# Eight merge-gate tiles as two seven-product block steps inside the second attention, with sums and scalings on GpSimd

## The chip, the cores and the metric

One NeuronCore of a Trainium2 chip runs the whole kernel as one program. The metric is the time of one execution on the device, in microseconds; the kernel's time is the median of three runs. The engines are named as in the profile: PE is TensorE (matmuls), PEld its weight loads, DVE is VectorE, ACT is ScalarE, POOL is GpSimd, and SP is SyncE, which here only issues DMAs.

## The reference

The layer works on 512 tokens of width 1024: a half-weighted feed-forward stage, a token mixer, a second half-weighted feed-forward stage, each between norms. The change lies in the token mixer, which projects the normed tokens `h` once with a wide matrix `w_in`, runs two attentions on slices of the result, and merges them with two gates:

```python
proj = h @ w_in
q_n, kv_n, g_n, qkv_d, merge = jnp.split(proj, np.cumsum(sizes)[:-1].tolist(), axis=-1)
...
o_nsa = nsa_attention(...)                       # first attention, 8 heads of 64
o_dil = dilated_attention(q, k, v)               # second attention, 3 groups of 4 heads of 64
y_nsa = o_nsa.reshape(B, S, Q_NSA) @ w_nsa_o
y_dil = o_dil.reshape(B, S, DIL_OUT) @ w_dil_o
g_a, g_b = jnp.split(merge, 2, axis=-1)          # 1024 columns each
y = jax.nn.sigmoid(g_a) * y_nsa + jax.nn.sigmoid(g_b) * y_dil
return y @ w_mix_out
```

In the second attention each of the three groups has its own window and dilation (128 by 1, 512 by 4, 2048 by 16). The groups' outputs are combined with weights that come from all three softmax denominators:

```python
for gidx, (window, dil) in enumerate(DIL_CONFIGS):
    o, lse = banded_attention(strided(q), strided(k), strided(v), 1, window // dil, dil, slopes[gidx])
    ...
w = jax.nn.softmax(jnp.stack(lses), axis=0)
o = jnp.sum(w[..., None] * jnp.stack(outs).astype(jnp.float32), axis=0)
```

## The kernel before

Every fp32 matrix product is done as three fp32r matmuls: each operand is split into a high part (ACT casts it, L149) and a rest (DVE subtracts, L150), and `mm3` issues high x high, high x rest and rest x high (L172 to L174). For a weight the parts are the tiles `whi` and `wlo`, three buffers each; the tokens' parts, with the feature in the partitions, are `xhl_t` (views `xh`, `xl`, `xht`, `xlt`). Weights come from DRAM into `raw` tiles of 1 MB, of which there are three. PSUM has eight banks under four tags: three S, two T, one V, two F. Tiles of 128x512 have tags of their own with a fixed count (SP 11, x 8, PT 8, Q, KA, KB and V 4 each, ring 3, W and of 2). The order of instructions on each engine is set when the kernel is built: a list planner takes the instructions in program order as their priority and places each on its engine by a cost model; `issue_after(i)` keeps an instruction behind instruction `i`. SP's queue of DMAs is in such an order too, and so is POOL's.

The mixer runs in these steps.

`nsa` is the first attention: 16 pairs of head and branch; scores on PE, softmax on DVE and ACT, the scaling of the probabilities mostly on POOL (L1180), transposes and value products on PE. The heads' outputs are folded (`fold`, L1207) into four tiles `of`, and each is split at once into `oh` and `ol`, which are the stationary-side input of the output projection later.

`merge_unit(u)` computes one of 16 tiles of the merge gates: 128 gate columns by 512 tokens, 8 x 3 matmuls of 512 columns, a copy from PSUM to a `ring` tile, a store to DRAM (`gdram`). Two units share one `raw` load. Units are fillers: PE does them where it would wait. Six come in `nsa`, one after each of five attentions of `dil`, one after the first value projection, two after the second, and the last two in the value loop.

`dil` is the second attention. It has six turns (three groups, two pairs of heads each). A turn projects q and k (two times 24 matmuls of 512 columns, `project`); a turn later `attend` does its scores (PE, S banks), the softmax (L938 on DVE, L939 on ACT) and keeps the probabilities. After the last turn the softmax statistics go through DRAM to change their layout, and the factors `fac` and `gf` of each group come out of them, the last ones again through DRAM (`fdram`). Meanwhile PE projects the values: group 0 in four products of 256 columns, groups 1 and 2 together in four banks S, S, T, T; copies and subtractions (L1439, L1440) keep them as high part and rest. Then comes the value loop over 12 items (head, group): scale the four probability tiles on DVE (L1476), transpose them on PE into a T bank (L1481, L1494), split them into PT tiles, multiply with the values (L1508, L1509, L1516), add up on DVE (L1520), fold.

The tail of `mixer` loops over the eight output tiles `d`: the projection of the first attention (12 matmuls of 512 columns), that of the second (6), both gates loaded from `gdram`, a sigmoid on ACT (L1606), the products with the gates on DVE (L1607), their sum and its split. The last product of the mixer (`down`, with `w_mix_out`) reads these.

The feed-forward stages already do block steps of the kind that the change adds: a 2x2x2 block product in seven products P1 to P7 in place of eight, with the token sums T1 to T4 shared by all steps, and weight sums per step.

## Time and profile before

| what | us |
|---|---|
| median of three runs | 1111.24 |
| the three runs | 1109.87, 1111.65, 1111.24 |
| the profiled execution | 1111.52 |
| its span in the profile | 1109.7 |
| PE busy | 1093.3 |
| DVE busy | 882.2 |
| ACT busy | 641.4 |
| POOL busy | 183.4 |

Busy times are sums of instructions over the span. A matmul's own time in the rows is longer than its share of the engine, since matmuls are pipelined; the distance from one start to the next is what PE needs for one. In the rows of an engine's timeline the columns are start, duration, engine, line, operation, output and inputs, shape and count, and in brackets the idle time before it and what ended that. In the rows of groups the columns after the count are the busy time, the mean in ns, and the idle time before with what ended it. A stretch shows its bounds, its length and for each engine the busy time and the number of instructions.

### The profile page before, as it was taken

What the parts mean: (1) busy time and instruction counts of PE and PEld (TensorE: products, weight loads), DVE (VectorE), ACT (ScalarE), POOL (GpSimd) and SP (SyncE); (2) the same over time, 40 slices, a digit from 0 to 9 for tenths busy, and PEclk for the clock granted to TensorE, in tenths of its full rate; (3) what the DMA queues carried; (4) which work ended last, traced back from release to release, by engine and by line L of the source; (5) the groups of instructions that cost most, each with busy time, mean ns of one, the idle gap of its engine ahead of it and who ended that gap; (6) DMA issues with size and microseconds to landing.
All of it is one profiled execution on the core that took longest, in us unless ns stands there. A gap on an engine that the chain in (4) does not pass through costs nothing.

```text
span 1109.7 us, 18548 instructions
## 1 busy us (share of the span) xinstructions
PE 1093.3 (99%) x6878; PEld 973.6 (88%) x6878; DVE 882.2 (79%) x1555; ACT 641.4 (58%) x1152; POOL 183.4 (17%) x264
## 2 busy tenths in 40 slices
PE   9999999999999999999999999999999999999997
PEld 7899999988789887777888998887989999997886
DVE  6989999998786989786554646976888999989575
ACT  7455555567565778685564625644435555567452
POOL 0444444310020056463000000001000000000001
PEclk9999999999999999999999999999999999999999
DMA  9899999999863497996213415383334444578862
GB/s 351 250 274 315 274 320 292 302 322 333 299 214 115 145 276 245 285 247 159 67 67 134 146 66 179 128 306 109 105 114 138 128 138 126 143 222 291 285 185 103
DMA packets 81050, 227.53 MB, mean 205 GB/s; under 512 B 12448, under 2 KB 15552, under 8 KB 77504
## 3 DMA queue, kind: packets, MB, share of 16 engines
q1 hardware_dynamic: 64592, 174.18, 46.8%
q0 software_dynamic: 16224, 51.91, 18.6%
q8 instruction: 54, 0.88, 0.3%
q14 instruction: 36, 0.29, 0.1%
q10 hardware_dynamic: 144, 0.26, 0.1%
HBM read 191.66 MB, written 57.72 MB: 225 GB/s over the span
## 4 chain that ended last, share of the span: by engine, by line
PE 79%; DVE 9%; ACT 4%; DMA 4%; issue 2%; POOL 1%; SPq 0%; DVEq 0%; POOLq 0%; ACTq 0%
PE pb_F L173 9%; PE pb_F L172 9%; PE pb_F L174 9%; PE pb_S L173 7%; PE pb_S L174 7%; PE pb_S L172 7%; PE pb_T L174 5%; PE pb_T L173 5%; PE pb_T L172 5%; DVE wlo L150 2%; PE pb_V L172 2%; DMA SP_s<-odram 2%; PE pb_V L173 2%; PE pb_V L174 2%; PE pb_V L1204 1%
## 5 line engine op out<-in xcount | busy, mean ns | idle before, releaser
L150 DVE TENSOR_TENSOR wlo<-raw,whi 128x1024 fp32r<-128x1024 f32 (+2 forms) x210 | 248.1, 1185 | 120.9 <-ACT whi L149 116.7
L149 ACT CAST whi<-raw 128x1024 fp32r<-128x1024 f32 (+2 forms) x210 | 213.7, 1018 | 162.2 <-PE pb_F L173 39.0
L172 PE MATMUL pb_F<-xhl_t,whi 128*128 128x512 f32 (+1 forms) x432 | 151.8, 351 | 0.9 <-DVE Q_s L1440 0.5
L174 PE MATMUL pb_F<-xhl_t,wlo 128*128 128x512 f32 (+1 forms) x432 | 150.6, 349 | 0.0
L173 PE MATMUL pb_F<-xhl_t,whi 128*128 128x512 f32 (+1 forms) x432 | 150.5, 348 | 0.0
L193 POOL TENSOR_TENSOR rs_t<-rs_t,mhalf_t 128x1 f32<-128x1 f32 x20 | 13.3, 664 | 553.3 <-DVE rs_t L189 553.3
L172 PEld LDWEIGHTS pb_F<-xhl_t,whi 128*128 128x128 f32 x432 | 81.3, 188 | 10.8 <-DVE xhl_t L250 1.0
L174 PEld LDWEIGHTS pb_F<-xhl_t,wlo 128*128 128x128 f32 x432 | 81.3, 188 | 9.9 <-DVE wlo L150 0.5
L173 PEld LDWEIGHTS pb_F<-xhl_t,whi 128*128 128x128 f32 x432 | 81.3, 188 | 9.2 <-issue 0.2
L172 PE MATMUL pb_S<-xhl_t,whi 128*128 128x256 f32 (+1 forms) x280 | 83.3, 297 | 0.0
L173 PE MATMUL pb_S<-xhl_t,whi 128*128 128x256 f32 (+1 forms) x280 | 83.1, 297 | 0.0
L174 PE MATMUL pb_S<-xhl_t,wlo 128*128 128x256 f32 (+1 forms) x280 | 83.1, 297 | 0.0
L1180 POOL TENSOR_SCALAR SP_s<-SP_s,st_t 128x384 f32<-128x384 f32 (+2 forms) x48 | 51.1, 1203 | 85.1 <-DVE st_t L1116 55.2
L172 PE MATMUL pb_T<-xhl_t,whi 128*128 128x256 f32 x200 | 55.3, 277 | 0.0
L173 PE MATMUL pb_T<-xhl_t,whi 128*128 128x256 f32 x200 | 55.3, 276 | 0.0
L174 PE MATMUL pb_T<-xhl_t,wlo 128*128 128x256 f32 x200 | 55.3, 276 | 0.0
L172 PEld LDWEIGHTS pb_S<-xhl_t,whi 128*128 128x128 f32 x280 | 52.6, 188 | 2.2
L174 PEld LDWEIGHTS pb_S<-xhl_t,wlo 128*128 128x128 f32 x280 | 52.6, 188 | 2.2
L173 PEld LDWEIGHTS pb_S<-xhl_t,whi 128*128 128x128 f32 x280 | 52.6, 188 | 2.2
L149 ACT CAST whi<-tmp_t 128x1024 fp32r<-128x1024 f32 x36 | 36.4, 1052 | 30.4 <-DVE tmp_t L525 23.5
L150 DVE TENSOR_TENSOR PT_s<-pb_T,PT_s 128x512 fp32r<-128x512 f32 (+1 forms) x72 | 39.2, 560 | 8.8 <-ACT PT_s L149 7.8
L382 POOL DMA_DIRECT2D PT_s<-in_d_dram x44 | 39.0, 977 | 34.2 <-DMA PT_s<-in_d_dram 18.6
(866 smaller groups left out, 3351.4 us busy)
## 6 DMA issues: line engine op xcount, KB each, us to landing
raw<-in_gu_dram SPq DMA_DIRECT2D x64, 512.0 KB, 5.0
raw<-tdram SPq DMA_DIRECT2D x40, 512.0 KB, 5.1
raw<-in_w_in_dram SPq DMA_DIRECT2D x19, 1024.0 KB, 4.9
PT_s<-in_d_dram POOLq DMA_DIRECT2D x66, 256.0 KB, 7.2
raw<-in_d_dram SPq DMA_DIRECT2D x30, 512.0 KB, 4.5
tdram<-in_d_dram POOLq DMA_DIRECT2D x18, 768.0 KB, 10.1
tdram<-PT_s POOLq DMA_DIRECT2D x44, 256.0 KB, 5.7
CP_s<-in_gu_dram SPq DMA_DIRECT2D x20, 512.0 KB, 4.2
```

Of the source, the lines that this page charges most:

```text
L149: self.last_cast = self.nc.scalar.copy(dsthi, src).ins
L150: self.last_sub = self.nc.vector.tensor_sub(dstlo, src, dsthi.bitcast(F32)).ins
L172: mm(out, lhi, rhi, start=start, stop=False, skip_group_check=skip)
L173: mm(out, lhi, rlo, start=False, stop=False, skip_group_check=skip)
L174: self.last_mm = mm(out, llo, rhi, start=False, stop=stop, skip_group_check=skip).ins
L193: nc.gpsimd.tensor_tensor(out=r, in0=v, in1=self.mhalf, op=OP.pow)
L382: add = lambda dst, src: put(dst, src, accum_op=OP.add)
L1180: self.last_pool = nc.gpsimd.tensor_scalar(pp, pp, st[:, 1, t:t + 1], None, op0=OP.mult).ins
L1204: self.nc.tensor.matmul(out[:, kk * P:S], v, pp, start=first and kk == 0 and pi == 0, stop=False, skip_group_check=True)
```

## The change

Units 8 to 15 (the second gate) are no longer done one by one. They become two lots of four units. A lot is a block step: two halves of the inner dimension by two halves of 256 gate columns by two halves of 256 tokens, in seven products of 24 matmuls of 256 columns each. `STEPS` says how many products stand behind each of the six attentions: 3, 3, 1 for the first lot, 4, 2, 1 for the second. The token sums T1 to T4 are made once (`mix_token_sums`), on DVE with a part on POOL; the weight sums of a lot are made on POOL. Units 6 and 7 and the first attention's output projection for the first four tiles `d` (`EARLY`) become pieces of six matmuls, handed out in the value loop; the first gate of these four tiles is loaded and applied there. The scaling of the 48 probability tiles of the second attention moves from DVE, where it stood in the value loop, to POOL, all of it ahead of the value projections in program order. The q and k weights are loaded per turn (128 columns of each) in place of per group. The splits of the first attention's outputs move from `nsa` to just before the value loop. Several tiles change their tags.

```diff
+STEPS = (3, 3, 1, 4, 2, 1)
+NSA_UNITS = 6
+PLAIN_UNITS = 8
+EARLY = 4
...
-GROUPS += [[(c + 256 * g, 256)] for g in range(3) for c in (C_QD, C_KD)]
+GROUPS += [[(C_QD + P * j, P), (C_KD + P * j, P)] for j in range(6)]
...
@@ nsa
-                        of = self.slot("of")
+                        of = self.slot("x")
...
-                        hi, lo = self.slot("x", F32R), self.slot("x", F32R)
-                        self.split(hi, lo, of)
-                        self.oh.append(hi)
-                        self.ol.append(lo)
+                        self.oh.append(of)
...
+    def unit_steps(self, u):
+        if u % 2 == 0:
+            self.mraw = self.wcols([(C_GA + u * P, 2 * P)])
+        w = self.wsplit(self.mraw[:, :, (u % 2) * P:(u % 2 + 1) * P], [KT, P])
+        b = self.bank("F")
+        for k in range(KT):
+            self.mm3(b, w[0][:, k], w[1][:, k], self.xh[k], self.xl[k], k == 0, k == KT - 1)
...
+            if k % 2:
+                yield
+
+    def mix_token_sums(self, names):
...
+        def less(dst, a, t):
+            nc.vector.tensor_sub(dst, part(self.xht, *a), t)
+            nc.vector.tensor_add(dst, dst, part(self.xlt, *a))
...
+        if "T1" in names:
+            self.top_tags = ["SP"] * 11 + ["V"] * 4 + ["x"]
...
+            with self.tc.issue_after(self.last_pool), self.tc.issue_after(self.last_fold):
+                nc.gpsimd.tensor_sub(s, part(self.xlt, 0, hi), part(self.xlt, 0, lo))
+                nc.vector.tensor_sub(t, part(self.xht, 0, hi), part(self.xht, 0, lo))
+                nc.vector.tensor_add(t, t, s)
+            keep("T1", t)
+            return
+        t2 = new()
+        less(t2, (4, hi), self.t1)
+        keep("T2", t2)
+        t3 = new()
+        with self.tc.issue_after(self.last_pool):
+            nc.gpsimd.tensor_sub(t3, part(self.xht, 4, hi), part(self.xht, 0, hi))
+            nc.gpsimd.tensor_add(t3, t3, part(self.xlt, 4, hi))
+            nc.gpsimd.tensor_sub(t3, t3, part(self.xlt, 0, hi))
+        less(t2, (4, lo), t2)
+        keep("T4", t2)
+        keep("T3", t3)
...
+    def unit_blocks(self, u, b):
+        st["P5"], st["P6"] = [self.sbt("tmp", [P, 4, 256], bufs=2) for _ in range(2)]
+        with self.tc.issue_after(self.last_pool):
+            nc.gpsimd.tensor_add(st["P5"], b[0, 1], b[1, 1])
+            nc.gpsimd.tensor_sub(st["P6"], st["P5"], b[0, 0])
+            nc.gpsimd.tensor_sub(b[0, 1], b[0, 0], b[0, 1])
...
+            if name == "P6":
+                nc.gpsimd.tensor_sub(b[1, 0], b[1, 0], st["P6"])
+        def run(name):
...
+                st[key] = self.bank(dict(X="T", Y="V", Z="T")[key])
+            for n in range(2):
+                c = slice(n * P, (n + 1) * P)
+                for j in range(4):
+                    self.mm3(st[key][:, n * 256:(n + 1) * 256], hi[:, j, c], lo[:, j, c], self.tops[top][0](j),
+                             self.tops[top][1](j), start and n == 0 and j == 0, False, True)
...
+        def finish(name):
+            if name in ("P1", "P6", "P7", "P4"):
+                v = st[name + "c"] = self.slot("ring")
+                nc.scalar.copy(v, st["X"])
+            for key in dict(P2="Y", P7="Z", P6="Z", P3="Y").get(name, ""):
+                v = st[dict(P2="P1c", P7="P7c", P6="P6c", P3="P6c")[name]]
+                nc.vector.tensor_add(v, st[key], v)
...
+        for name in ("P1", "P2", "P5", "P6", "P3", "P7", "P4"):
+            prep(name)
+            run(name)
+            finish(name)
+            yield
...
@@ dil
+        load(0, 0)
+        load(0, 1)
+        for n, t in enumerate(turns):
+            pairs[t] = project(*t)
+            if n == 0:
+                lot(8)
+                self.mix_token_sums(("T1",))
+            if n == 1:
+                load(1, 0)
+                self.mix_token_sums(("T2", "T3", "T4"))
+            if n:
+                attend(*turns[n - 1], *pairs.pop(turns[n - 1]))
+                blocks(STEPS[n - 1])
+            if n == 1:
+                load(1, 1)
+            if n == 3:
+                load(2, 0)
+                lot(12)
+                load(2, 1)
+        attend(*turns[-1], *pairs.pop(turns[-1]))
+        blocks(STEPS[-1])
...
+        for hh in range(4):
+            for g in range(3):
+                for t in range(NT):
+                    pr = probs[g][hh][t]
+                    nc.gpsimd.tensor_scalar(pr, pr, gf[g][:, t, hh:hh + 1], None, op0=OP.mult)
...
-            for t in range(NT):
-                nc.vector.tensor_scalar(pr[t], pr[t], gf[g][:, t, hh:hh + 1], None, op0=OP.mult)
...
+        for _ in range(2):
+            next(fillers)
+        early_gates()
+        for n, of in enumerate(self.oh):
+            hi, lo = self.slot("x", F32R), self.slot("SP", F32R)
+            with self.tc.issue_after(kept[0]), self.tc.issue_after(kept[1]):
+                self.split(hi, lo, of)
...
+            with self.tc.issue_after(self.last_value if n == len(items) else self.last_trans):
+                for _ in range(2 if n == 0 else 1):
+                    next(fillers)
...
@@ mixer
+        def pieces():
+            for u in range(NSA_UNITS, PLAIN_UNITS):
+                yield from self.unit_steps(u)
+            for d in range(EARLY):
+                if d % 2 == 0:
+                    w = first_weights(d)
+                b = self.bank("F")
+                for k in range(4):
+                    self.mm3(b, w[0][:, k, c], w[1][:, k, c], self.oh[k], self.ol[k], k == 0, k == 3)
+                    if k == 3:
+                        times(d, 0, b, self.last_cast)
+                    if k % 2:
+                        yield
```

More of the change, by code (lines that the diff above doesn't have):

```diff
@@ L1212, in fold @@
         nc.scalar.copy(dst[rows], far)
-        nc.vector.tensor_add(dst[rows], near, dst[rows])
+        self.last_fold = nc.vector.tensor_add(dst[rows], near, dst[rows]).ins
     def nsa(self, fillers, sums):
@@ L1320, in merge_unit @@
         self.nc.sync.dma_start(self.gdram[u], s)
-    def dil(self, fillers):
+    def unit_steps(self, u):
[5 more added lines that the diff above has]
+            self.mm3(b, w[0][:, k], w[1][:, k], self.xh[k], self.xl[k], k == 0, k == KT - 1)
+            if k == KT - 1:
+                s = self.slot("ring")
+                self.nc.scalar.copy(s, b)
+                self.nc.sync.dma_start(self.gdram[u], s)
+            if k % 2:
+                yield
@@ L1323, in dil @@
+    def dil(self, fillers, early_gates):
         nc = self.nc
@@ L1379, in attend @@
                 else:
-                    pt = self.slot("SP" if (g == 1 and hh < 3) else ("CB" if (g, hh) == (2, 3) else "CP"))
+                    pt = self.slot("x" if (g == 1 and hh < 3) else ("CB" if (g, hh) == (2, 3) else "CP"))
                     b = self.bank("S")
@@ L1391, in attend, with load, blocks, lot @@
                 nc.sync.dma_start(self.sdram[g - 1].rearrange("(n r) c -> n r c", r=4), st.rearrange("p t h s -> p t (h s)"))
-        prev = None
-        for g in range(3):
-            for j in range(2):
-                cur = (g, j) + project(g, j)
-                if prev is not None:
-                    attend(*prev)
-                    fillers()
-                prev = cur
-        attend(*prev)
+        def load(g, j):
+            raws[g, j] = self.wcols([(C_QD + 256 * g + P * j, P), (C_KD + 256 * g + P * j, P)])
+        lots = []
+        def blocks(n):
+            for _ in range(n):
+                if next(lots[0], 0) == 0:
+                    lots.pop(0)
+                    next(lots[0])
+        def lot(u):
+            lots.append(self.unit_blocks(u, self.unit_loads(u)))
+        turns = [(g, j) for g in range(3) for j in range(2)]
+        pairs = {}
+        load(0, 0)
[19 more added lines that the diff above has]
+        blocks(STEPS[-1])
         nat = [stats[0]]
@@ L1452, in dil @@
             vt[0].append(keep(b[:, 0:256], 0, t))
-        fillers()
+        kept = self.kept
         banks = [self.bank(tag) for tag in "SSTT"]
@@ L1552, in mixer @@
         self.fdram = tc.dram_tile([2, S, 4], F32, name="fdram")
-        units = iter(range(16))
+        units = iter(range(NSA_UNITS))
         def fill(n):
@@ L1570, in mixer, with gate, times, first_weights @@
         self.nsa(fill_half, sums)
-        self.dil(fill(1))
+        wn, wd = a["w_nsa_o"], a["w_dil_o"]
+        gates = [[None, None] for _ in range(KT)]
+        def gate(d, i, tag):
+            g = gates[d][i] = self.slot(tag)
+            nc.sync.dma_start(g, self.gdram[d + 8 * i])
+        def times(d, i, b, behind):
+            g = gates[d][i]
+            with self.tc.issue_after(behind):
+                nc.scalar.activation(g, g, AF.Sigmoid)
+            nc.vector.tensor_mul(g, g, b)
+        def first_weights(d):
+            r = self.pool.tile([P, 4, 256], F32, name="raw", tag="raw", bufs=3)
+            nc.sync.dma_start(r, wn[d // 2])
+            return self.wsplit(r, [4, 256])
+        def pieces():
+            for u in range(NSA_UNITS, PLAIN_UNITS):
+                yield from self.unit_steps(u)
+            w = None
+            for d in range(EARLY):
+                if d % 2 == 0:
+                    w = first_weights(d)
+                b = self.bank("F")
+                c = slice((d % 2) * P, (d % 2 + 1) * P)
+                for k in range(4):
[4 more added lines that the diff above has]
+                        yield
+        self.dil(pieces(), lambda: [gate(d, 0, "KB") for d in range(EARLY)])
         behind = self.last_exp, self.last_cast
-        fill(16)()
-        wn, wd = a["w_nsa_o"], a["w_dil_o"]
         ytags = [t for t in ("PT", "Q", "KA", "V") for _ in range(SLOTS[t])]
-        ys, gates = [], []
+        ys = []
         def load_gates(d):
             if d < KT:
-                gates.append([self.slot("KB" if d < 2 else "SP") for _ in range(2)])
-                for g, u in zip(gates[d], (d, 8 + d)):
-                    nc.sync.dma_start(g, self.gdram[u])
+                for i in range(d < EARLY, 2):
+                    gate(d, i, "SP")
         for d in range(GATES_AHEAD):
@@ L1587, in mixer @@
         for d in range(KT):
[L1588 to L1594 removed]
+            if d % 4 == 0:
+                rd = self.raw(wd[d // 4], [2, 512])
+                w_d = self.wsplit(rd, [2, 512])
+            if d % 2 == 0 and d >= EARLY:
+                w = first_weights(d)
             b1, b2 = self.bank(), self.bank()
[L1596 to L1598 removed]
+            if d >= EARLY:
+                c = slice((d % 2) * P, (d % 2 + 1) * P)
+                for k in range(4):
+                    self.mm3(b1, w[0][:, k, c], w[1][:, k, c], self.oh[k], self.ol[k], k == 0, k == 3)
             c = slice((d % 4) * P, (d % 4 + 1) * P)
```

81 lines of the change are left out of this document (51 added, 30 removed).

## The prediction

> **What bounds the kernel now.** I read the page first, then stretches of the mixer, then TensorE's waits, then single rows.
>
> ```profile
> span 1109.7 us, 18548 instructions
> PE 1093.3 (99%) x6878; PEld 973.6 (88%) x6878; DVE 882.2 (79%) x1555; ACT 641.4 (58%) x1152; POOL 183.4 (17%) x264
> PE 79%; DVE 9%; ACT 4%; DMA 4%; issue 2%; POOL 1%; SPq 0%; DVEq 0%; POOLq 0%; ACTq 0%
> ```
>
> PE is busy 99% of the span and 79% of the chain that ended last. The stretches say whether that holds where the change acts (columns: stretch, its length, busy time of PE, weight load, DVE, ACT, POOL with instruction counts, granted clock, DMA share, GB/s). The last two are a stretch of nothing but 128x512 gate and projection matmuls and one of nothing but 128x256 block products of the second feed-forward stage.
>
> ```profile
> 512.00:537.00 25.00, 25.00 (x121) 20.82 (x121) 13.06 (x17) 11.44 (x19) 0.00 (x0) 1.00 0.32 103
> 518.90:572.00 53.10, 53.10 (x250) 44.35 (x249) 28.30 (x65) 30.15 (x64) 2.09 (x4) 1.00 0.26 90
> 619.00:637.00 18.00, 17.47 (x123) 16.34 (x123) 12.37 (x57) 10.40 (x31) 0.00 (x0) 1.00 0.41 116
> 637.00:659.00 22.00, 22.00 (x95) 22.00 (x95) 11.40 (x36) 5.66 (x9) 0.00 (x0) 1.00 0.28 99
> 671.00:705.00 34.00, 33.35 (x200) 27.80 (x199) 27.67 (x63) 18.40 (x39) 0.00 (x0) 1.00 0.50 155
> 705.00:735.00 30.00, 30.00 (x134) 24.81 (x133) 28.38 (x43) 19.22 (x31) 0.00 (x0) 1.00 0.60 200
> 539.02:555.14 16.12, 16.12 (x72) 13.33 (x71) 7.92 (x19) 8.61 (x23) 0.51 (x1) 1.00 0.36 121
> 860.00:960.00 100.00, 100.00 (x885) 100.00 (x884) 94.35 (x121) 55.25 (x78) 0.00 (x0) 1.00 0.46 134
> ```
>
> Through the second attention (512 to 637), the value loop (671 to 705) and the output projections, PE runs without a hole, at clock 1.00, while DVE and ACT have a third to a half of their time free up to 637, and DVE is 81% and 95% taken after 671. The list of waits of PE from 500 to 760 is short:
>
> ```profile
> PE pb_V L1204 <- DVE of_s L1213: 1.1, 1, 1.1
> PE pb_F L172 <- DVE Q_s L1440: 0.5, 1, 0.5
> PE pb_F L172 <- ACT W_s L149: 0.4, 1, 0.4
> PE pb_S L1516 <- DVE PT_s L150: 0.2, 1, 0.2
> ```
>
> So there is 2.2 us of waiting to win; anything more must come from fewer matmul columns.
>
> **The change, part by part.**
>
> *Eight gate tiles as block steps.* A 128x512 matmul costs 16.12 / 71 = 0.227 us, a 128x256 one 100 / 885 = 0.113 us: half, so the smaller shape costs no extra. Before, units 8 to 15 are 8 x 24 = 192 matmuls of 512 columns, 43.6 us. After, two lots of seven products, each 2 x 4 x 3 = 24 matmuls of 256 columns: 336 x 0.113 = 38.0 us, 2.71 us a product. PE saves 5.6 us with these means, and 5.4 (48 x 0.113) counted by columns, which I take. PE has no holes here, so that is 5.4 on the path. The other matmuls (units 6 and 7, the output projection of the first four tiles) move only.
>
> *What feeds them.* Each product needs a split of 128x1024 (ACT whi, DVE wlo), 14 instead of 8; four ring copies per lot; four adds per lot with one PSUM input.
>
> ```profile
> L149 ACT CAST whi<-raw 128x1024 fp32r<-128x1024 f32 x20 | 21.0, 1050 | 41.4 <-PE pb_F L173 23.8 <-issue 16.8 <-ACT CP_s L939 0.4
> L150 DVE TENSOR_TENSOR wlo<-raw,whi 128x1024 fp32r<-128x1024 f32 x20 | 24.5, 1224 | 40.5 <-ACT whi L149 40.5
> L1319 ACT COPY ring_s<-pb_F 128x512 f32<-128x512 f32 x6 | 3.5, 589 | 0.1
> L150 DVE TENSOR_TENSOR x_s<-raw,x_s 128x512 fp32r<-128x512 f32 x4 | 2.8, 691 | 0.9 <-ACT x_s L149 0.9
> 502.84 0.62 ACT L149 CAST x_s<-of_s 128x512 fp32r<-128x512 f32 x1 [0.76 <-DVE of_s L1213]
> ```
>
> The token sums T1, T2, T4 are two DVE operations each of 1024 columns (6 x 1.22 = 7.3), and the four kept sums eight splits of 512 columns (DVE 8 x 0.69 = 5.5, ACT 8 x 0.62 = 5.0). They fall with the first lot. From the stretch 518.9 to 572: DVE had 28.3; two unit splits leave (-2.4), six product splits (7.3), sums (7.3 + 5.5) and three adds (2.1) come: 48.1 of 53.1, 91%. ACT: 30.15 - 3.3 + 6.3 + 1.8 + 5.0 = 40.0. In the row from 860 to 960 DVE is 94% taken and PE still has no hole, so I take nothing for the cover itself; T4, 3.8 of the 48.1, isn't wanted before the third gap. The second lot has no token sums and is lighter.
>
> *Sums on GpSimd.* Per lot three operations of 128x1024 before P5 and P6 and one before P3; T1 needs one more, T3 three. No large two-input operation of POOL is in the trace. The nearest row is the scaling of probabilities:
>
> ```profile
> 495.25 2.72 POOL L1180 TENSOR_SCALAR SP_s<-SP_s,st_t 128x384 f32<-128x384 f32 x3 [1.42 <-ACT SP_s L939]
> L1180 POOL TENSOR_SCALAR SP_s<-SP_s,st_t 128x256 f32<-128x256 f32 x16 | 17.3, 1081 | 0.0
> L1180 POOL TENSOR_SCALAR SP_s<-SP_s,st_t 128x128 f32<-128x128 f32 x16 | 15.0, 938 | 0.0
> 513.85 0.33 SPq L887 DMA_DIRECT2D raw<-in_w_in_dram  x1
> 522.71 0.33 SPq L887 DMA_DIRECT2D raw<-in_w_in_dram  x1
> raw<-in_w_in_dram SPq DMA_DIRECT2D x11, 1024.0 KB, 4.9
> 536.71:538.74 2.03, 2.03 (x18) 1.00 0.00 0
> ```
>
> 768 columns in 2.72 us are 3.5 ns a column, 3.6 us for 1024 (an estimate, with one input; twice that with two, 7.2, is the upper bound, and the lower one 1.22, DVE's price). I take 3.6, the nearest row. The lot's second raw tile can't load before the first projection has split its own (the slot of 522.71), and lands 4.9 later, near 528. P5's sum is then ready at 531.6, its split at 534; P5 starts after the first attention (scores end at 538.74) and P1 and P2 (5.4): 544. So 10 us cover it. If T3's three stand in front on POOL's queue, it is 528 + 14.4 + 2.3 = 544.7, 0.7 late. Behind POOL's sums on its queue wait the zero fills of the next keys, wanted only some 10 us later.
>
> The Trainium skill (GPSIMD Engine Reference, Elementwise — side-by-side cycle accounting) gives about 2.6 cycles of 1.2 GHz an element for a two-input add: 2.2 us by that page (an estimate), which would make POOL earlier; no row of this trace shows such an operation.
>
> *DVE and GpSimd at the same time.* Here they overlap for the first time in this stage. A split during a POOL operation:
>
> ```profile
> 423.13 1.49 DVE L150 TENSOR_TENSOR wlo<-raw,whi 128x1024 fp32r<-128x1024 f32 x1
> 422.88 3.12 POOL L1180 TENSOR_SCALAR SP_s<-SP_s,st_t 128x384 f32<-128x384 f32 x3 [4.32 <-ACT ring_s L1319]
> ```
>
> 1.49 against 1.22, and 3.12 against 2.72: both a little longer. Eight POOL operations against the first lot at 0.27 each make DVE 2.2 longer, 50.3 of 53.1. The upper end is that they exclude each other (first rival). I take 0.6 us of PE waits for it, nearer to the measured overlap.
>
> The Trainium skill (SBUF — State Buffer, Who interferes with whom) says that a DVE instruction with two SBUF inputs and a GpSimd instruction that reads SBUF exclude each other for the whole instruction. In the rows above the split overlapped the scaling almost wholly and lost 0.27 us, so the trace doesn't bear that out in full.
>
> *Scaling on GpSimd.*
>
> ```profile
> L1476 DVE TENSOR_SCALAR SP_s<-SP_s,fac_t x16: 278/346/349, 629.5 to 642.0; 128x256 f32<-128x256 f32 x12, 128x128 f32<-128x128 f32 x4
> 618.81 0.28 PE L933 MATMUL pb_S<-KB_s,Q_s 128*128 128x128 f32 x1
> 632.41 1.68 SPq L1430 DMA_DIRECT2D gf_t<-fdram  x2
> ```
>
> 48 such DVE operations leave (0.28 to 0.35 us, in DVE's free time, so nothing on the path except the 0.5 us wait of PE for DVE's Q_s, which stood among them: -0.5, with 0 as the other end). On POOL they are 36 of 128 columns and 12 of 256: at most 36 x 0.94 + 12 x 1.08 = 46.8 us; at 3.5 ns a column, 7680 columns, 27 us. The factors are loaded about 17 us after the last attention's scores, as now (618.8 to 632.4, two loads and their landing). In these 17 us and after stand the last product (2.7), the value projections (10.9 and 22.0) and two pieces (2.7): POOL has a lead of 21 us before the first transpose. The value loop then takes some 2.8 us an item against at most 3.9 on POOL: 46.8 against 21 + 11 x 2.8 = 52, so POOL isn't late even at the upper price: 0.
>
> *Fillers moved.* Units 11 to 13, now between the value projections and the value loop, go. What they cover: the copies that clear the banks.
>
> ```profile
> 659.31 0.40 PE L172 MATMUL pb_F<-xhl_t,whi 128*128 128x512 f32 x1
> 660.73 0.65 ACT L1439 CAST V_s<-pb_T 128x256 fp32r<-128x256 f32 x2
> L1520 DVE TENSOR_TENSOR ring_s<-pb_S,ring_s 128x256 f32<-128x256 f32 x31 | 11.8, 417 | 0.5 <-PE pb_S L1516 0.2
> ```
>
> The last copy ends at 661.4 and its subtraction 0.4 later, 2.5 us after the projections end at 659.3; two pieces of six matmuls (2.7) stand there after: 0 to 0.5, I take 0.2. In the value loop 12 pieces of 1.36 (16.3 us) replace about 17 us of fillers, and DVE gets one split and up to four gate products more: 27.67 + 1.2 + 2.8 = 31.7 of 34. I take 0.4 of waits. The end of the loop (fold, split, last projection) keeps as cover the remaining output tiles' matmuls (four of 2.7). The attention output's splits leave the first attention (4 x 0.69 of DVE) for the projections' stretch, where DVE is half free: 0, with the 1.1 us wait for of_s as the other end.
>
> *DMAs.* Eight block loads of 512 KB replace four of 1024; q and k loads are regrouped at equal size; eight stores of equal size; the gate loads come earlier for four tiles. All on SP's queue at 0.26 to 0.5 DMA share: 0.
>
> Sum: -5.4 - 0.5 + 0.6 + 0.2 + 0.4 = -4.7 us. The profiled execution took 1111.5 (span 1109.7), 0.3 above the median, so 1106.8 for it and 1111.24 - 4.7 = **1106.5** for the median.
>
> **The rivals.**
>
> 1. *Slower: DVE and GpSimd exclude each other in the first lot.* POOL's eight operations are 8 x 3.6 = 29 us; DVE's with two SBUF inputs are 12 splits, six sums, eight kept parts: 14.7 + 7.3 + 5.5 = 27.5. Together 56.5 in 53.1: 3.4 over if all else overlaps, and 48.1 + 29 - 53.1 = 24 if DVE waits for each. It decides once PE loses more than 5.4 + 2.2. In the middle, 13.7: 1111.2 - 5.4 + 13.7 = 1119.5. Against it: the 0.27. Chance 0.08. The Trainium skill (SBUF — State Buffer, Who interferes with whom) states this rule.
> 2. *The value loop becomes DVE's.* 31.7 of 34 with chains through ACT: if each of 12 items waits 0.3, 3.6 us, and 1111.2 - 5.4 + 3.6 = 1109.4, the edge of no change. For it: the 81% now; against it: 95% after 705 with no hole. Chance 0.14, half of it faster.
> 3. *GpSimd is late for P5.* At 7.2 us a sum with T3 in front: 528 + 28.8 + 2.3 = 559, 15 late, of which the next projection (10.9) can fill most: 4 us, 1109.8. Chance 0.10, no change.
> 4. *The block steps don't save,* because another engine ends the stage: excluded by the stretches, except through 1 to 3. A slower result from a wait that I don't name: 0.06.
>
> **How the numbers follow.** Main case 0.62, faster. A measurement tells 0.2%, 2.2 us, from no change, so faster means under 1109.0. Faster 0.62 + 0.07 = 0.69; same 0.07 + 0.09 = 0.16; slower 0.08 + 0.06 + 0.01 = 0.15. The main case alone spans 1104.2 (5.4, 0.5 and the 1.1 us all won, no waits) to 1109. The range 1104.2 to 1112.0 takes in rivals 2 and 3 and leaves out rival 1.
>
> **What would show it.** PE's rows at 0.113 in 14 runs of 24, about 38 us; PE without holes from 512 to 637 and the span shorter by about that much already before 637, relative to the work done. POOL's 1024-column rows at 2 to 4 us; DVE's splits beside them under 1.6. Wrong if PE shows waits over 3 us on wlo, T sums, tmp_t or SP_s, if splits last 3 us beside POOL, or if transposes wait for POOL.

## The result: slower by 0.7%

The changed kernel took 1118.13, 1118.22 and 1119.29 us, against a median of 1111.40 for the kernel before: a ratio of 1.0067, 95% interval 1.0047 to 1.0087. The forecast was 1106.5, with a range from 1104.2 to 1112.0. On another chip, five executions had a median of 1117.85 against 1110.85, ratio 1.0065 (1.0053 to 1.0078). A fourth execution on the first chip, the profiled one, ran from 888 us on at a granted clock of 0.16, took 2177.43 us and is left out, so the lines of the changed kernel below come from the profile taken on the other chip (1118.17 us, span 1115.9). Helper lines have moved by four: L154 is the split on DVE, L176 to L178 are `mm3`, L936 and L937 the scores, L942 the softmax on DVE, L1368 to L1370 T3's three sums on POOL, L1399 P3's sum.

The page of the changed kernel:

```profile
span 1115.9 us, 18925 instructions
PE 1092.9 (98%) x7022; PEld 980.2 (88%) x7022; DVE 901.2 (81%) x1535; ACT 652.1 (58%) x1166; POOL 255.2 (23%) x324
PE 70%; DVE 12%; ACT 6%; DMA 5%; POOL 3%; issue 3%; SPq 0%; DVEq 0%; POOLq 0%; ACTq 0%
```

PE has as much busy time as before (1092.9 against 1093.3) in a span that is 6.2 longer. The stretches that the prediction used, now of the changed kernel:

```profile
512.00:537.00 25.00, 24.80 (x117) 20.15 (x115) 20.97 (x20) 12.87 (x21) 14.82 (x6) 1.00 0.17 57
518.90:572.00 53.10, 46.98 (x261) 41.65 (x260) 41.17 (x72) 30.05 (x60) 12.80 (x8) 0.94 0.14 45
671.00:705.00 34.00, 32.53 (x189) 28.35 (x188) 25.06 (x56) 21.00 (x43) 17.30 (x27) 1.00 0.30 101
705.00:735.00 30.00, 28.69 (x138) 23.44 (x138) 26.99 (x49) 19.05 (x33) 0.00 (x0) 1.00 0.63 220
```

The second line holds the loss: PE stood for 6.1 of 53.1 us, and the clock there has a mean of 0.94. DVE is 78% busy in it: the mean gives no hint that DVE is the cause. PE's waits from 500 to 760, without two entries of 0.4 and 0.3 in the first attention:

```profile
PE pb_S L936 <- DVE dst_t L942: 6.1, 1, 6.1
PE pb_S L178 <- DVE wlo L154: 1.3, 1, 1.3
PE pb_T L1636 <- DVE SP_s L154: 0.7, 1, 0.7
PE pb_T L1636 <- POOL CP_s L1576: 0.4, 1, 0.4
PE pb_V L1650 <- ACT SP_s L153: 0.4, 1, 0.4
```

One wait makes most of the list. PE wants the fourth score bank of the second attention, there are three S banks, and the first comes free only with the softmax on DVE. PE's rows around it (start, duration):

```profile
538.23 0.28 PE L937 MATMUL pb_S<-KB_s,Q_s 128*128 128x256 f32 x1
544.62 0.58 PE L936 MATMUL pb_S<-KA_s,Q_s 128*128 128x256 f32 x1 [6.12 <-DVE dst_t L942]
545.86 0.41 PE L177 MATMUL pb_T<-xhl_t,whi 128*128 128x256 f32 x1
549.49 0.39 PE L176 MATMUL pb_T<-xhl_t,whi 128*128 128x256 f32 x1
549.70 0.29 PE L177 MATMUL pb_T<-xhl_t,whi 128*128 128x256 f32 x1
```

From 544.62 to 549.70, behind the hole, matmuls of 256 columns start 0.213 apart instead of 0.12 (17 steps from 545.86 to 549.49): PE runs at half clock. And why the softmax was late, on DVE and then on POOL:

```profile
529.51 0.68 DVE L920 TENSOR_TENSOR KA_s<-pb_F,KB_s 64x512 fp32r<-64x512 f32 x1 [1.16 <-ACT KA_s L919]
530.93 5.50 DVE L154 TENSOR_TENSOR SP_s<-CP_s,SP_s 128x512 fp32r<-128x512 f32 x2
536.47 1.23 DVE L1346 TENSOR_TENSOR CP_s<-xhl_t,CP_s 128x1024 f32<-128x1024 f32 x1
540.28 2.05 DVE L1347 TENSOR_TENSOR CP_s<-CP_s,xhl_t 128x1024 f32<-128x1024 f32 x1
543.79 0.42 DVE L942 CUSTOM_DVE_ANT_0 PT_s<-pb_S,W_s 128x256 f32<-128x256 f32 x1
```

```profile
527.35 3.25 POOL L1368 TENSOR_TENSOR CP_s<-xhl_t 128x1024 f32<-128x1024 f32 x1 [8.83 <-DVE SP_s L154]
530.68 2.40 POOL L1369 TENSOR_TENSOR CP_s<-CP_s,xhl_t 128x1024 f32<-128x1024 f32 x1
533.16 2.72 POOL L1370 TENSOR_TENSOR CP_s<-CP_s,xhl_t 128x1024 f32<-128x1024 f32 x1
538.91 2.34 POOL L1399 TENSOR_TENSOR raw<-raw,tmp_t 128x1024 f32<-128x1024 f32 x1 [3.02 <-DVE wlo L154]
```

Two splits of 0.69 took 5.50 together (the row merges one of 2.70 and one of 2.88). The second ends 0.55 behind POOL's L1370 (535.88). The sum L1347 takes 2.05 instead of 1.22 and ends 1.08 behind L1399 (541.25). By contrast, an instruction that reads one of its inputs from PSUM (L920, 529.51) takes its usual 0.68 while L1368 runs from 527.35 to 530.60. So an instruction of DVE with both inputs in SBUF waits for the sum that POOL is doing, and the profile counts that wait as its busy time.

**The reckoning.** I cut the trace at the first score matmul of the second attention and at the first transposes behind the mixer, in the kernel before and in the changed one:

```profile
536.71 0.28 PE L932 MATMUL pb_S<-KA_s,Q_s 128*128 128x256 f32 x1
763.72 1.32 PE L243 MATMUL pb_S<-ident_t,tmp_t 128*128 128x128 f32 x8 [0.25 <-DVE tmp_t L238]
```

```profile
536.93 0.28 PE L936 MATMUL pb_S<-KA_s,Q_s 128*128 128x256 f32 x1
769.89 1.32 PE L247 MATMUL pb_S<-ident_t,tmp_t 128*128 128x128 f32 x8 [0.17 <-DVE tmp_t L242]
```

Work is the length less PE's bracketed idle times in it:

| | length | waits of PE | work |
|---|---|---|---|
| before | 227.0 | 1.3 | 225.7 |
| changed | 233.0 | 9.1 | 223.9 |
| changed, all sums on DVE (below; 537.90 to 762.72) | 224.8 | 3.3 | 221.5 |

At full clock the work is 225.7 - 221.5 = 4.2 less; half clock gives 2.4 of it back (223.9 - 221.5). The hole costs 6.1 and the other waits are 1.6 more than before (9.1 - 6.1 - 1.3, from unrounded figures): -4.2 + 2.4 + 6.1 + 1.6 = +5.9, of the 233.0 - 227.0 = 6.0. Ahead of the cut the changed execution is 0.2 longer (536.93 against 536.71), and from the end of the cut to the last matmul both take 339.3. Together this is the 6.2 between the two spans, 1109.7 and 1115.9; the times of the two executions, 1111.52 and 1118.17, differ by 0.5 more, which lies outside the spans. The work without half clock can be checked on the run with T3 on DVE below, in which the clock stayed up: 221.3.

### The profile page after: what moved, and what is told of

Same layout as the page of the kernel before. It is cut to its first block, busy times and chain, and to the rows that moved or that the text cites. A ratio compares the mean times of both kernels' runs of the same rounds, so it can differ in the third digit from the quotient of the medians.

```text
span 2175.2 us, 18925 instructions
## 1 busy us (share of the span) xinstructions
PE 2152.9 (99%) x7022; PEld 1870.0 (86%) x7022; DVE 906.3 (42%) x1535; ACT 654.0 (30%) x1166; POOL 258.1 (12%) x324
## 4 chain that ended last, share of the span: by engine, by line
PE 88%; DVE 5%; ACT 3%; POOL 2%; DMA 1%; issue 1%; DVEq 0%; POOLq 0%; SPq 0%; ACTq 0%
PE pb_S L178 9%; PE pb_S L176 9%; PE pb_S L177 9%; PE pb_F L176 8%; PE pb_F L177 8%; PE pb_F L178 8%; PE pb_T L176 8%; PE pb_T L177 8%; PE pb_T L178 8%; PE pb_V L177 4%; PE pb_V L176 4%; PE pb_V L178 4%; DVE wlo L154 1%; POOL PT_s L1576 1%; ACT whi L153 1%
## 5 line engine op out<-in xcount | busy, mean ns | idle before, releaser
L154 DVE TENSOR_TENSOR wlo<-raw,whi 128x1024 fp32r<-128x1024 f32 (+2 forms) x212 | 252.2, 1194 | 594.3 <-ACT whi L153 591.9
L176 PE MATMUL pb_F<-xhl_t,whi 128*128 128x512 f32 (+1 forms) x368 | 156.6, 426 | 0.4 <-DVE xhl_t L254 0.2
L178 PE MATMUL pb_F<-xhl_t,wlo 128*128 128x512 f32 (+1 forms) x368 | 155.8, 423 | 0.0
L178 PE MATMUL pb_S<-xhl_t,wlo 128*128 128x256 f32 (+1 forms) x280 | 133.0, 475 | 0.0
L177 PE MATMUL pb_S<-xhl_t,whi 128*128 128x256 f32 (+1 forms) x280 | 132.8, 474 | 0.0
L176 PE MATMUL pb_S<-xhl_t,whi 128*128 128x256 f32 (+1 forms) x280 | 132.8, 474 | 0.0
L178 PEld LDWEIGHTS pb_F<-xhl_t,wlo 128*128 128x128 f32 x368 | 99.9, 271 | 7.5 <-DVE wlo L154 0.5
L176 PEld LDWEIGHTS pb_F<-xhl_t,whi 128*128 128x128 f32 x368 | 99.5, 270 | 7.7 <-DVE xhl_t L254 1.0
L178 PEld LDWEIGHTS pb_S<-xhl_t,wlo 128*128 128x128 f32 x280 | 102.8, 367 | 2.2
L177 PEld LDWEIGHTS pb_S<-xhl_t,whi 128*128 128x128 f32 x280 | 102.4, 366 | 2.2
L176 PEld LDWEIGHTS pb_S<-xhl_t,whi 128*128 128x128 f32 x280 | 102.4, 366 | 2.2
L178 PE MATMUL pb_T<-xhl_t,wlo 128*128 128x256 f32 x216 | 103.5, 479 | 0.0
L177 PE MATMUL pb_T<-xhl_t,whi 128*128 128x256 f32 x216 | 103.1, 477 | 0.0
L176 PE MATMUL pb_T<-xhl_t,whi 128*128 128x256 f32 x216 | 103.0, 477 | 0.0
L176 PE MATMUL pb_T<-SP_s,whi 128*128 128x256 f32 x176 | 85.2, 484 | 0.0
L178 PE MATMUL pb_T<-SP_s,wlo 128*128 128x256 f32 x176 | 84.8, 482 | 0.0
L178 PEld LDWEIGHTS pb_T<-xhl_t,wlo 128*128 128x128 f32 x216 | 84.5, 391 | 0.0
L176 PEld LDWEIGHTS pb_T<-xhl_t,whi 128*128 128x128 f32 x216 | 84.4, 391 | 0.0
```

Of the source, the lines that this page charges most:

```text
L154: self.last_sub = self.nc.vector.tensor_sub(dstlo, src, dsthi.bitcast(F32)).ins
L176: mm(out, lhi, rhi, start=start, stop=False, skip_group_check=skip)
L177: mm(out, lhi, rlo, start=False, stop=False, skip_group_check=skip)
L178: self.last_mm = mm(out, llo, rhi, start=False, stop=stop, skip_group_check=skip).ins
```

## The experiments

There were three theories. **A**, exclusion: POOL's sums hold back DVE, so the softmax comes late and PE waits for it. **B**, queue order: DVE has too much work in front of the softmax, whatever POOL does. **C**: most of the loss lies behind 640 us, where POOL scales the probabilities. Each run's kernel is the changed one with the edit shown; the times of the kernel before on the same chips were 1110.85 (first four runs), 1109.95 (next four), 1110.58 (next three) and 1111.05 (last).

**The changed kernel again.**

> The changed kernel once more, for a profile at full clock to set the others against. Theory A (exclusion): the three T3 sums on GpSimd (528.4 to 536.9) hold back a VectorE split of two SBUF inputs for nearly 5 us, the first softmax of the second attention starts late, and TensorE stands 6.1 us at its fourth score bank; behind that hole the 256-column matmuls run at 0.213 instead of 0.113 us for some 5 us. Theory B (queue order): VectorE simply has too much in front of that softmax, whatever GpSimd does. Theory C: most of the loss lies behind 640 us, where GpSimd scales the probabilities. Expected of all three: about 1118.5; the hole 5.5 to 6.5 us by A and B, and what is left (7.4 lost, 5.4 forecast as saved, so 12.8 to explain, of which the hole and its clock are some 8.5) in places still to be found.

Measured 1117.85; its rows are the ones above. C falls with the reckoning: 8.5 of what was lost lie between 538 and 550.

**T3 later.**

```diff
-self.mix_token_sums(("T2", "T3", "T4"))        # ahead of attend(0, 0)
+self.mix_token_sums(("T2", "T4"))
...
+self.mix_token_sums(("T3",))                   # behind attend(0, 0)
+    with self.tc.issue_after(self.last_soft):  # around T3's three sums
```

> T3's three sums stay on GpSimd, but are issued only behind the last softmax of the first attention half pair; VectorE's work in front of the first softmax stays as it was. A: the stretched split goes back to 0.69 us, TensorE's wait at the fourth score bank falls from 6.1 to 0.5 to 2, the clock stays at 1.00 there, and the time falls by 5 to 8 to 1111 to 1113.5. B: VectorE has the same instructions in front of the softmax, so at least 4 us of the wait stay and the time falls by less than 2.5. C: within 2 us of the changed kernel.

Measured 1117.99, ratio 1.0068 (1.0055 to 1.0081), the hole again 6.1. It tells nothing on A or B: the sums started at 527.80, as before. `issue_after` orders instructions in the plan; on the chip POOL waited for no softmax and began as soon as DVE's split had freed T3's tile.

**T3 on DVE.**

```diff
-nc.gpsimd.tensor_sub(t3, part(self.xht, 4, hi), part(self.xht, 0, hi))
+nc.vector.tensor_sub(t3, part(self.xht, 4, hi), part(self.xht, 0, hi))
...                                             # and T3's other two
```

> T3's three sums on VectorE instead of GpSimd, called at the same place: 3 x 1.22 = 3.7 us more on VectorE, no large GpSimd sum beside the splits there (one is left, 2.34 us, behind them). A: 4.8 us of standing still are swapped for 3.7 us of work, so the wait falls by 1 to 2 us and the time by 1 to 4 (the clock's dip shortens with it), unless the sums fall behind the softmax in VectorE's order. B: 3.7 us more work in front of the softmax, so the wait grows or stays and the time is 1118 to 1122. C: within 2 us of the changed kernel.

Measured 1113.43, ratio 1.0026 (1.0016 to 1.0035): 4.4 less, though DVE got 3.7 of work in front of the softmax. B is refuted, as far as load alone goes. A hole of 2.4 is left, with P3's sum on POOL beside it; one DVE row and one POOL row of this run:

```profile
538.76 3.30 DVE L1347 TENSOR_TENSOR CP_s<-CP_s,xhl_t 128x1024 f32<-128x1024 f32 x1
```

```profile
537.73 3.25 POOL L1399 TENSOR_TENSOR raw<-raw,tmp_t 128x1024 f32<-128x1024 f32 x1 [18.88 <-issue]
```

Each is longer than alone, DVE's 1.22 by 2.1 and POOL's 2.34 by 0.9: each waited for the other's.

**T2, T3 and T4 all later.**

```diff
-self.mix_token_sums(("T2", "T3", "T4"))        # ahead of attend(0, 0)
+self.mix_token_sums(("T2", "T3", "T4"))        # behind it; T2 and T3 issued behind its softmax
```

> T2, T3 and T4 (VectorE's and GpSimd's part) all issued behind the last softmax of the first attention half pair; their first use is the fourth block (P6) in the second gap. A and B both: TensorE's wait at the fourth score bank goes to below 1 us, the clock stays up, and the time falls by 6 to 9 to 1109.5 to 1112.5; if P6 then waits for T2, 1 to 3 us of it come back at the fourth block. A differs from B only beside the run with T3 alone moved. C: within 2 us of the changed kernel.

Measured 1117.49, ratio 1.0064 (1.0051 to 1.0077). The first half of the expectation held, the wait at the score bank fell to 0.2, but the time didn't: a hole of 5.7 opened 10 us later, where T3's sums now ran (they wait for their tile here). PE's wait, DVE's rows and POOL's:

```profile
PE pb_F L178 <- DVE wlo L154: 5.7, 1, 5.7
```

```profile
545.75 3.44 DVE L1347 TENSOR_TENSOR CP_s<-CP_s,xhl_t 128x1024 f32<-128x1024 f32 x1
549.72 4.33 DVE L1462 TENSOR_SCALAR W_s<-dm_s 128x128 f32<-128x128 f32 x4
```

```profile
544.85 3.27 POOL L1369 TENSOR_TENSOR CP_s<-xhl_t 128x1024 f32<-128x1024 f32 x1 [3.72 <-DVE CP_s L1346]
551.50 2.34 POOL L1371 TENSOR_TENSOR CP_s<-CP_s,xhl_t 128x1024 f32<-128x1024 f32 x1
```

The hole goes with POOL's sums. Even four small scalings with one input (L1462, 0.75 together in the run with all sums on DVE) took 4.33, until POOL's last sum ended at 553.84.

**One more sum on POOL.**

```diff
 nc.gpsimd.tensor_sub(t3, part(self.xht, 4, hi), part(self.xht, 0, hi))
+nc.gpsimd.tensor_sub(t3, part(self.xht, 4, hi), part(self.xht, 0, hi))
```

> The changed kernel with the first of T3's three sums on GpSimd issued twice (the same values are written again); nothing else changes on any engine, so GpSimd works four times in a row where it worked three times. Exclusion, one instruction at a time: one more of VectorE's instructions without an operand in PSUM meets a GpSimd sum and waits up to 2.4 us for it, TensorE's wait at the fourth score bank grows from 6.1 to 8 to 9 us, and the time by 2 to 3.5 (the clock stays low a little longer) to 1120 to 1121.5. If VectorE were only overbooked (queue order), GpSimd's fourth sum would cost nothing: 6.1 us and 1117.9.

Measured 1120.32 (four executions, 1116.95 to 1123.02), ratio 1.0090 (1.0071 to 1.0109). The time alone proves little: the executions lie 6 us apart, the interval overlaps that of the changed kernel, and the profiled one was the fastest. Its rows are clear. The wait grew by 2.1, and the next instruction of DVE in line became a stretched one too:

```profile
PE pb_S L936 <- DVE dst_t L942: 8.2, 1, 8.2
```

```profile
529.44 5.50 DVE L154 TENSOR_TENSOR SP_s<-CP_s,SP_s 128x512 fp32r<-128x512 f32 x2
534.98 3.30 DVE L1346 TENSOR_TENSOR CP_s<-xhl_t,CP_s 128x1024 f32<-128x1024 f32 x1
```

PE, DVE and ACT have the same instructions in the same order here, so the 2.1 us are POOL's doing. In the stretch of the reckoning only 1.0 of them is left (234.0 against 233.0), because less of the work behind this hole fell into half clock (see the last section).

**No sums on POOL.**

```diff
-nc.gpsimd.tensor_...                           # T1, T3, P5, P6, P7 and P3: all sums of the block steps
+nc.vector.tensor_...
```

> All sums of the block steps on VectorE: T1's, T3's three, and both lots' four (12 of 1.22 us = 14.6 us, five or six of them ahead of the first softmax in question); the scaling of the probabilities stays on GpSimd. Exclusion: nothing waits 2 us any more in 505 to 545, so VectorE's instructions stand at 1.22 and 0.69 throughout; against the run with T3 alone on VectorE (a wait of 2.4 us left) 2.1 us of standing still go and up to 1.2 us of work come before the softmax: 0.5 to 2 us of wait at the fourth score bank, 1111.5 to 1113.5. If it is VectorE's mere load that counts, the wait is 4 us or more and the time 1116 or more.

Measured 1110.06, ratio to the kernel before 1.0002 (0.9993 to 1.0010): by the ratios 0.63%, 7.0 us, below the changed kernel, better than expected. The wait at the score bank is 0.6, and L1347 is back at 1.22:

```profile
PE pb_S L936 <- DVE dst_t L942: 0.6, 1, 0.6
PE pb_T L1193 <- DVE PT_s L154: 0.9, 1, 0.9
```

```profile
539.52 1.22 DVE L1347 TENSOR_TENSOR CP_s<-CP_s,xhl_t 128x1024 f32<-128x1024 f32 x1
```

DVE is 99% busy from 520 to 550 here, and PE hardly waits: DVE's load was never enough to make the hole.

**A block ahead of the attention.**

```diff
+blocks(1) if n == 1 else None
 attend(*turns[n - 1], *pairs.pop(turns[n - 1]))
-blocks(STEPS[n - 1])
+blocks(STEPS[n - 1] - (n == 1))
```

> The first block (P1) is called ahead of the second attention's first half pair instead of behind it; all sums stay on GpSimd. TensorE has 35 matmuls of 0.113 us = 4.0 us to do before it comes to the fourth score bank; VectorE is as late as before. If hole and clock are both the cost of that one wait: it falls from 6.1 to about 2.1 us, the clock stays up (the run with a hole of 2.4 us kept 1.00), and the time falls by 4.0 + 2.8 = 6.8 to about 1111. If VectorE stays behind for longer (it works off its backlog until 550), the wait comes back at a later place, and the time stays above 1115.

Measured 1118.47, ratio 1.0079 (1.0066 to 1.0092): the wait comes back, as the second half of the expectation had it. The matmuls were done ahead, but with them the plan put P5's split, the next keys and a split of T4 ahead of the softmax, which began at 547.59 instead of 543.79; the wait became 6.8.

**Scaling on DVE.**

```diff
-nc.gpsimd.tensor_scalar(pr, pr, gf[g][:, t, hh:hh + 1], None, op0=OP.mult)
+nc.vector.tensor_scalar(pr[t], pr[t], gf[g][:, t, hh:hh + 1], None, op0=OP.mult)   # ahead of each transpose
```

> The changed kernel with the scaling of the probabilities back on VectorE, ahead of each transpose as before the change (16 of 0.35 and 32 of 0.28 us, 14 us in all), GpSimd idle there; the order on TensorE is the same. If the scaling on GpSimd costs (a wait of 0.4 us at the first transposes, VectorE's splits up to 0.2 longer beside it), the time falls by up to 1 us. If VectorE bounds the loop over values (17 to 19 us busy in 20 from 700 to 740 now), its 14 us come on top of it and the time rises by 3 to 9 us. I expect the second, +3 to 1121, as 680 to 740 has some 8 us of VectorE idle to hide part of it.

Measured 1117.79, ratio 1.0067 (1.0053 to 1.0080): no difference to the changed kernel, against my expectation of +3. DVE did all of the scalings between 649 and 666, where it has time, before the value loop and not in it, so the run doesn't tell what they would cost inside the loop (first line: this run, second: the changed kernel; DVE is the third busy time, POOL the fifth):

```profile
660.00:680.00 20.00, 19.65 (x89) 18.40 (x89) 13.53 (x37) 6.96 (x14) 0.00 (x0) 1.00 0.27 92
```

```profile
660.00:680.00 20.00, 19.60 (x89) 18.49 (x88) 8.34 (x15) 6.61 (x13) 20.00 (x26) 1.00 0.26 90
```

The scaling on POOL neither gains nor costs. In the changed kernel DVE's splits beside its instructions of 0.6 us took at most 1.40 instead of 1.22.

**The hole filled with work.**

```diff
+b = self.bank("V")                             # ahead of the fourth score bank
+for k in range(54): self.nc.tensor.matmul(b[:, 0:256], self.xh[k % 8][:, 0:P], self.xh[k % 8][:, 0:256], ...)
```

> The changed kernel with 54 matmuls of 256 columns (of values that are overwritten, 54 x 0.113 = 6.1 us) between the third and the fourth score bank of the second attention's first half pair, so TensorE works through the time in which it stood; VectorE and GpSimd as in the changed kernel. If the slow stretch behind the hole (22 matmuls at 0.213 instead of 0.118, 2.2 us) is the clock's answer to the standing still, it goes: wait below 1 us, clock 1.00 from 540 to 560, and the time falls by 2 to 3 to 1115 to 1116. If the slow matmuls come from something else (operands late, the banks), they stay and the time is 1117.5 to 1118.5.

Measured 1116.61, ratio 1.0059 (1.0047 to 1.0072). The clock stayed up (first line: this run, second: the changed kernel; the clock is the third figure from the end):

```profile
545.00:550.00 5.00, 5.00 (x45) 5.00 (x43) 4.12 (x11) 4.96 (x16) 0.52 (x1) 1.00 0.00 0
```

```profile
545.00:550.00 5.00, 5.00 (x26) 5.00 (x26) 4.73 (x15) 4.96 (x16) 0.52 (x1) 0.53 0.00 0
```

45 matmuls against 26 in the same 5 us: the slow stretch is the clock's answer to PE standing still. The time fell by 1.2 between the medians and not by 2 to 3, and the intervals of the two ratios overlap. In the stretch of the reckoning 0.8 is left of the 2.4 (232.2 against 233.0): the fourth score bank's matmul came 0.2 later after the first score matmul (7.9 against 7.7), and a wait of 0.5 came behind it; where the rest went is open.

**The lots' sums on POOL, the rest on DVE; and the same with `EARLY` = 2.**

```diff
-nc.vector.tensor_add(st["P5"], b[0, 1], b[1, 1])    # of the run with no sums on POOL
+nc.gpsimd.tensor_add(st["P5"], b[0, 1], b[1, 1])    # and P6's and P7's; T1, T3 and P3 stay on DVE
...
-EARLY = 4                                            # second run only; the loop then stops
+EARLY = 2                                            # asking for pieces when they are used up
```

> As the run with all sums on VectorE, but with each lot's first three sums on GpSimd again (the first lot's ran there from 510.9 to 519.6, when VectorE was busy two thirds of the time and mostly with instructions that read PSUM); T1's, T3's and P3's stay on VectorE. With the sums on VectorE, TensorE waited 0.9 us at 506.8 for a split behind them; that wait goes, the 0.6 us at the fourth score bank stays, and the time falls by 0.5 to 1 to 1109 to 1109.6, 0.05 to 0.1% below the kernel before. Rival: the first lot's GpSimd sums hold back splits again, and the time rises by 1 or more.

> As the run with each lot's first three sums on GpSimd, with only two of the four gated output tiles pulled into the loop over values instead of four (the other two are made in the output loop, as all were before the change). VectorE is busy 17 to 18 of each 20 us from 700 to 740, and TensorE waits 1.1 us there for the split of the first output weights; with less of the output's gate work there the wait goes, if VectorE's load is its cause: 1 us less, 1108 to 1109. If the early tiles are TensorE's fill in the last steps of the loop, taking them away opens waits there instead: 1110 to 1113.

Measured 1110.76, ratio 0.9998 (0.9987 to 1.0010), and 1111.36, ratio 1.0006 (0.9997 to 1.0015). In the first the wait of 0.9 went as expected, but the time stayed within the spread: no version beats the kernel before measurably. In the second the 1.1 us wait went, and others came at 698 to 703, with the clock down behind them.

**POOL's sums in short instructions.**

```diff
-nc.gpsimd.tensor_sub(t3, part(self.xht, 4, hi), part(self.xht, 0, hi))
+for j in range(4): nc.gpsimd.tensor_sub(t3[:, j], part(self.xht, 4, hi)[:, j], part(self.xht, 0, hi)[:, j])
...                                             # T3's other two and P3's alike
```

> The changed kernel with T3's three sums and P3's sum cut into four instructions of 256 columns each on GpSimd (the same values; every other engine has the same instructions in the same order). If VectorE waits only for the GpSimd instruction that is running, the two splits that took 5.5 us together beside three instructions of 2.4 us wait 0.6 to 0.7 us each (1.4 us of work and about as much waiting: 2.5 to 3), the sum beside P3's takes 1.6 to 1.9 instead of 2.05, TensorE's wait at the fourth score bank falls from 6.1 to 2.5 to 3.5 us, the clock stays up or dips shortly, and the time falls by 4 to 6 to 1112 to 1114. If GpSimd keeps VectorE out until its whole row of sums is done, the 5.5 us, the 6.1 us and 1117.9 stay, or grow with the twelve starts.

Measured 1115.26, ratio 1.0037 (1.0024 to 1.0051). The two splits took 1.84 instead of 5.50, and the hole 3.4 instead of 6.1. The time fell by 2.6 and not by 4 to 6, since the clock still went down (541.6 to 548.4), which I had not expected of a hole this short:

```profile
531.07 1.84 DVE L154 TENSOR_TENSOR SP_s<-CP_s,SP_s 128x512 fp32r<-128x512 f32 x2
```

```profile
PE pb_S L936 <- DVE dst_t L942: 3.4, 1, 3.4
```

```profile
545.00:550.00 5.00, 5.00 (x31) 5.00 (x31) 3.85 (x10) 4.97 (x16) 0.00 (x0) 0.66 0.00 0
```

DVE waits for the GpSimd instruction that is running, not for the row of them. It is a smaller harm, not a remedy: T3's sums on POOL took longer (3.69, 5.75 and 3.78, against 3.25, 2.40 and 2.72). Four undisturbed pieces of 0.73 follow one another in some 2.8, and pieces that met a split or sum of DVE took 1.2 to 1.7.

## Why the prediction was wrong

*The step that failed* is "I take 0.6 us of PE waits for it, nearer to the measured overlap". It measured 8.5: the hole of 6.1 and 2.4 at half clock. The mechanism was the first rival's, to which I gave 0.08; that its 1119.5, from a loss of 13.7 in the middle of its bounds, came within 1.5 us of the result was luck, since the loss was 8.5 and other terms made up the rest.

The 0.27 was read beside another kind of POOL instruction: the row holds three scalings ("x3", 3.12 us together), and the split began 0.25 behind the first. POOL's sums last 2.3 to 2.4 undisturbed, and the splits and sums in the rows shown lost 0.8 to 2.2 beside them. Taken one by one, the rows give the price. An instruction of DVE that starts while a sum runs on POOL loses the rest of that sum less 0.14 us: the first of the two splits had 2.15 of L1369 ahead of it and lost 2.01, L1347 had 0.97 of L1399 ahead and lost 0.83, and all 63 such meetings with more than 0.2 us ahead that the traces show between 380 and 800 us fit within 0.02 (splits and sums of 128x512 and 128x1024, with 0.69 and 1.22 as their usual times). Beside scalings the loss is smaller: the split of 1.49 had 1.08 of the first scaling ahead of it and lost only 0.27. So I carried over the price beside one kind of instruction as a constant to another that is longer and holds DVE back almost to its end.

The Trainium skill (SBUF — State Buffer, Who interferes with whom) says that the first to issue holds the shared port pair for its whole instruction and the other blocks, and that an instruction of DVE with at most one SBUF input, outside the modes that use both ports, is not concerned. The runs agree with both where POOL does sums: 5.50 for two splits, 0.68 for L920. Beside POOL's scalings DVE did not block to the end of the instruction (the 0.27). I had weighed that rule against one row that couldn't decide it.

*"48.1 of 53.1"* for DVE, and from it *"so I take nothing for the cover itself"*, held without POOL's sums: DVE was 99% busy from 520 to 550, and the wait at the score bank was 0.6. But a mean over 53 us doesn't show where the load lies, and a stop of 5 us there finds no slack. The forecast asked whether an engine has time, and not whether the one instruction that PE waits for comes in time.

*Half clock* behind a hole is missing in the prediction, in the sum and in the rivals.

*5.4 from fewer columns* measured 4.2. In the stretch cut above, 336 more matmuls of 256 columns took the place of 192 of 512. Start to start (PE's rows of the run with T3 on DVE) a short one took 0.120 on average, not 0.113; a long one took 0.2315 before. 192 x 0.2315 - 336 x 0.120 = 4.1, nearly the 4.2. The 0.113 came from a stretch with nothing but short ones; the 96 short ones that the kernel before has in the same stretch take 0.12 already.

*Waits behind 640:* 0.2 + 0.4 - 0.5 were forecast. The 0.5 for Q_s went, as forecast. In its place and that of two small ones (0.4 and 0.2) stand 1.3 + 0.7 + 0.4 + 0.4: some 1.6 more than before, 1.5 more than forecast. They stand in the run with no sums on POOL too (1.1, 0.7, 0.4 and 0.4), and in the run with the scaling back on DVE, so neither of these is their cause. The second rival (value loop bound by DVE) is in that, at about half its price; that DVE's load is the cause of the 1.3 was not shown, since the run with less of it moved the wait.

*GpSimd late for P5* didn't happen: a sum lasted 2.3 to 3.3 (estimated 3.6), and the first lot's three before P5 and P6 were done by 520, since its weights were there at 510 and not near 528. The 2.2 that the prediction works out from the Trainium skill (GPSIMD Engine Reference, Elementwise — side-by-side cycle accounting) is nearer: undisturbed sums took 2.34 to 2.41. *Scaling as 0* was right: 38 us on POOL, a wait of 0.4 at the transposes, and no difference with it back on DVE.

Two of the signs of being wrong came in another form, both in the same place: PE did wait over 3 us, but for the softmax (dst_t), which the prediction's list of tiles lacks, and the splits took 2.70 and 2.88, where the sign was 3 and the forecast under 1.6. Without POOL's sums the block steps leave 4.2 less work and 2.0 more waits in the same stretch, which begins 1.0 to 1.2 later (537.70 and 537.90 against 536.71); whether 0 or 1 us of gain remains, these runs don't settle.

## What to carry to other kernels

Moving work to GpSimd isn't free time, even where both engines show idle shares: a VectorE instruction that read its inputs from SBUF waited for the GpSimd sum under way, so price each meeting at the rest of that instruction, look for the VectorE result that TensorE waits for next, and keep GpSimd's instructions short or away from it. VectorE did the same sum in half the time (1.22 against 2.34), so with 30 us of VectorE booked solid, adding the sums to it was still 7 us cheaper. TensorE's holes of 3.4 us and more cost their length and 1.4 to 2.8 us of half clock behind them (work above the 221.5 of the reckoning).

## What the runs showed of the hardware

DVE's wait for POOL doesn't show as idle time: DVE's busy time while its splits wait is full (9.88 of 10 us from 530 to 540 in the changed kernel; 9.85 with no sums on POOL, when it did 12 instructions there instead of 8), and only an instruction's own duration against its usual one gives it away.

Half clock followed holes of 3.4, 5.7, 6.1, 6.8 and 8.2 us and not one of 2.4. In the undisturbed traces the granted clock changed only at whole steps of 3.413 us, counted from where the trace first shows it (157 steps to the fall in the changed kernel, 160 in the run with T2, T3 and T4 later, 158 with a block first), and behind each of these holes it stayed down for 6.83 us, two steps, however long the hole was. So a longer hole can cost less at half clock: work resumed 6.4, 5.1 and 3.1 us before the clock came back behind the holes of 3.4, 6.1 and 8.2, and lost 2.8, 2.4 and 1.4 to it (the clock is the third figure from the end; the short sums, the changed kernel, one more sum):

```profile
541.55:548.38 6.83, 6.35 (x29) 6.35 (x30) 6.75 (x24) 6.78 (x22) 3.30 (x6) 0.50 0.00 0
```

```profile
542.88:549.71 6.83, 5.08 (x24) 5.09 (x25) 6.34 (x21) 6.76 (x19) 0.52 (x1) 0.50 0.00 1
```

```profile
541.52:548.35 6.83, 3.15 (x14) 3.15 (x15) 5.83 (x18) 5.28 (x11) 1.35 (x3) 0.50 0.00 1
```

The Trainium skill (TensorE: Matmul & The Clock Gate, Part 1) gives about 3.4 us of idling as what halves the clock, and as much sustained work to bring it back; these holes agree, though the clock fell 2.5 and 2.9 us into two of them (5.7 and 3.4), and the return took 3.1 to 6.4 us here. In the run with two early tiles, however, four waits of 0.29, 0.17, 0.63 and 0.43 within 5 us were followed by one step at half clock, which that figure doesn't explain. In the step ahead of it PE was busy 2.18 of 3.41 us with 12 matmuls (first line, then the step at half clock). In the run with T3 on DVE it was just as little busy in a step, but with 19 matmuls (last line), and the clock stayed up; what decides is open.

```profile
700.31:703.72 3.41, 2.18 (x12) 1.38 (x11) 3.41 (x9) 1.94 (x5) 0.00 (x0) 1.00 0.18 41
703.72:707.13 3.41, 3.41 (x11) 2.72 (x10) 1.78 (x7) 0.00 (x0) 0.00 (x0) 0.50 0.95 375
```

```profile
538.41:541.83 3.42, 2.16 (x19) 1.96 (x17) 3.39 (x2) 3.17 (x5) 3.09 (x2) 1.00 0.01 2
```
